# Two more pairs in the seven-product form in the down projection, and half of its loads on GpSimd's queue

## The chip, the cores and the metric

One core of a Trainium2 chip runs the whole kernel. The metric is the device time of one execution in microseconds (us), as a median of several runs. The engines are named as the profile names them: PE is TensorE's matmul, PEld its weight load, DVE is VectorE, ACT is ScalarE, POOL is GpSimd, SP is SyncE, which here only issues transfers. POOL issues transfers too.

## The reference, cut to what matters

One decoder layer over 256 tokens and 16 meta tokens with D_MODEL 2048: attention and retention heads from one input projection, an output projection, and a gated MLP with D_FF 5632. Only the MLP bears on this case. All of it is float32.

```
def conv_glu(u, w_gate, w_up, conv_w, w_down):
    g = u @ w_gate                      # then a causal depthwise conv of width 3
    ...
    return (jax.nn.silu(gc) * (u @ w_up)) @ w_down
```

`w_down` has 5632 rows and 2048 columns. Its product with the activations is the down projection, the last large product before the final norm.

## The kernel before, in words

Every large product runs on PE with each float32 operand split into a high and a low part of type fp32r: the high part is a cast (ACT, line 206, a copy into an fp32r tile), the low part is the difference (DVE, line 207, a subtraction). A product is then three matmuls, high by high, high by low and low by high (`triple`, lines 872 to 874). The 5632 rows of `w_down` are 44 blocks of 128, called k blocks.

**The gate and up stage** (loop over `f` in `range(NF)`, from line 794) makes the activations, one k block a step, and keeps their parts in `fhi` and `flo`. For the first `KP` = 2 x `NS` blocks the stage forms, after each odd `f`, four sums of the activations of two neighbouring blocks (lines 831 to 834), splits them, and stores three of them, high and low, to DRAM as `sd[p]` (384 KB, from POOL's queue, line 843). Between these steps it also prepares sums of the weights: `stage()` loads three blocks of a pair's weights (`ts`, 768 KB, POOL's queue, line 782), `sums()` makes two of the sums on DVE (lines 788 and 789) and stores both as `td[g, p]` (512 KB, POOL's queue, line 791), and stages the next. There are 2 x `NS` such steps. The staging tiles are the memory of `htok`, the residual, which is read back late in the stage, in halves.

**The down stage** (from line 927) works through two halves of the columns, `g` = 0 and 1, each of two blocks of 512 columns, for two halves of the tokens, 128 each. For two plain k blocks this takes 8 products of 128x128 by 128x512, that is 24 matmuls and two entries of prepared weights of 128x1024. For a pair of the first `KP` blocks, seven products do (a 2x2 by 2x2 scheme of Winograd's kind): 21 matmuls. A pair has four entries, called parts:

- `d`: two blocks of weights (128x1024), 2 products, one of which takes a stored sum of activations (`sf`)
- `u`: the two stored weight sums `td`, 2 products, both with `sf`
- `t`: a difference of what `d` and `td` loaded, made in place on DVE (line 218), 2 products
- `c`: one block of weights `sw` (128x512), 1 product

`down_order` mixes the parts with plain entries: a lead of plain entries (4 in the first half, 2 in the second), then the parts with the other plain entries spread between them, then a tail of plain entries (3, and 8 in the second half). With `NS` = 12 there are 12 pairs and 20 plain entries in each half. `NPL` is the number of plain pairs of blocks in one block of columns.

**Buffers and queues.** `ahead` loads up to 6 entries ahead and prepares (`prep`) up to 3 ahead in program order. Prepared weights lie in a ring of four: three buffers of `whi`/`wlo` and one of `wx`. Raw weights have five buffers. `sf` and `sw` have two each, for even and odd pairs. `load` issues four transfers for a pair, all from SP's queue: the two blocks of `d` (line 179), `sf` (line 180), `td` (line 181), `sw` (line 182). `keep` holds the marked instructions in program order; all others are placed by a scheduler that goes by its own timeline, so the order on each engine is fixed before the run but not by hand.

Small work for the residual is spread over the entries by `pump`: after the last part of a half, ten additions into `htok`; in the second half four products with the norm's weights (`weigh`, line 899) and one scaling of a norm tile (line 860), whose load `norm` is also from POOL's queue (line 855).

Of the kernel before, what the change touches and what calls it, by code (L numbers as in the profile page):

```python
# [10 lines left out]
F32 = mybir.dt.float32  # L11
# [29 lines left out]
NW = 512  # L41
# [3 lines left out]
LAM_INIT = 0.8 - 0.6 * math.exp(-0.3 * 0)  # L45
HK = KT // 2
HOLD = 6
NS = 12
KP = 2 * NS
NPL = (NF - KP) // 2  # L50
LEAD = [(4, 3), (2, HOLD + 2)]
# [44 lines left out]
def down_order():  # L96
# [3 lines left out]
    for g in range(2):  # L100
        plain = [("w", 2 * g + j, b) for j in range(2) for b in range(NPL)]
        parts = [("s", p, q) for p in range(NS) for q in PARTS]
        lead, tail = LEAD[g]
# [13 lines left out]
def trunk_kernel(ctx, tc, a, out):  # L117
    nc = tc.nc
# [23 lines left out]
    keep = tc.keep_in_program_order  # L142
# [18 lines left out]
    pools = {}  # L161
# [4 lines left out]
    def load(c):  # L166
        turn = (c - nw) % 5 if c >= nw else 0
        if turn == 3:
            t = pools["dn"].tile([P, D], F32, tag="sraw", name=f"raw{c}")
        elif turn == 4:  # L170
            t = big.tile([P, D], F32, tag="act1", name=f"raw{c}")
        else:
            t = wp.tile([P, D], F32, tag="raw", bufs=3, name=f"raw{c}")
        if c in mixed:
            g, p = divmod(mixed[c], NS)
            sf = big.tile([P, 6 * P], F32R, tag=f"act{2 + p % 2}a", name=f"sf{g}_{p}")
            sw = big.tile([P, NW], F32, tag=f"act{2 + p % 2}b", name=f"sw{g}_{p}")
            w = a["w_mix"][g, p]
            keep(nc.sync.dma_start(out=t[:, :2 * NW], in_=w[:, :2 * NW]))
            keep(nc.sync.dma_start(out=sf.bitcast(F32), in_=pools["sd"][p]))  # L180
            keep(nc.sync.dma_start(out=t[:, 2 * NW:], in_=pools["td"][g, p]))
            keep(nc.sync.dma_start(out=sw, in_=w[:, 2 * NW:3 * NW]))
            pools["sf"][g, p] = sf
            pools["sw"][g, p] = sw
        else:
            ins = nc.sync.dma_start(out=t, in_=chunks[c])
            if c >= nw:
                keep(ins)
        raw[c] = t

    def prep(hf):
# [18 lines left out]
        if c in mixed:  # L210
            g, p = divmod(mixed[c], NS)
            if s == "d":
# [75 lines left out]
    with tc.tile_pool(name="start", bufs=2) as st:  # L288
        acc = st.tile([P, 4, T], F32, name="acc", bufs=1)
        xrs, rws = [], []  # L290
        for c in range(4):
# [7 lines left out]
            for b, e in cuts:  # L299
                lead = c == 0 and b == 0  # L300
                (nc.scalar if lead else nc.sync).dma_start(
                    out=xr[:, b:e], in_=a["x"][:, 4 * c + b:4 * c + e])
# [140 lines left out]
    def gemm_q(idx, src, pumps):  # L443
        ps = unit(idx)
        for k, wh, wl in steps(idx, pumps):
            PE.matmul(ps[:, :NQ + 2], wh, src.cols(k, GO - 2, GL), start=(k == 0), stop=False)  # L446
            PE.matmul(ps[:, 4:NQ + 2], wh, src.cols(k, GL, GW), start=False, stop=False)  # L447
            PE.matmul(ps[:, 2:NQ + 2], wl, src.hi(k), start=False, stop=(k == KT - 1))  # L448
        edge = sp.tile([P, 2], F32, tag="edge", name=f"edge{idx}")
        S.copy(out=edge, in_=ps[:, 0:2])  # L450
        V.tensor_tensor(out=ps[:, 2:4], in0=ps[:, 2:4], in1=edge, op=ALU.add)
        return ps[:, 2:NQ + 2]

    def gemm_t(idx, src):
        ps = unit(idx)
        for k, wh, wl in steps(idx, 0):
            if k == KT - 1:
                PE.matmul(ps[:, :SEQ], wl, src.cols(k, GO + 2, GL), start=False, stop=False)
            PE.matmul(ps, wh, src.cols(k, GO + 2, GW), start=(k == 0), stop=(k == KT - 1))  # L459
            if k < KT - 1:  # L460
                PE.matmul(ps[:, :SEQ], wl, src.cols(k, GO + 2, GL), start=False, stop=False)  # L461
        return ps

    with ExitStack() as p1:
# [269 lines left out]
        for j in range(KT):  # L734
# [15 lines left out]
            for i in range(4):  # L750
                c = j * P + i * 32
                nc.sync.dma_start(
                    out=hd[:, c:c + 32].rearrange("(b t) f -> t b f", t=32),
                    in_=hb[i * 32:(i + 1) * 32].rearrange("t (b f) -> t b f", f=32))
# [9 lines left out]
    with ExitStack() as p2:  # L764
# [4 lines left out]
        fw = p3.enter_context(tc.tile_pool(name="fw", bufs=2))  # L769
        sd = [dp.tile([P, 6 * P], F32, name=f"sd{p}") for p in range(NS)]  # L770
        us = {}
        td = {}
        staged = []
        halfs = []
        order_g = [(g, p) for g in range(2) for p in range(NS)]

        def stage():
            n = len(td) + len(staged)
            if n < len(order_g):
                t = big.tile([P, 3, NW], F32, tag=f"htok{n % 2}", name=f"ts{n}")  # L780
                g, p = order_g[n]
                keep(nc.gpsimd.dma_start(out=t.rearrange("p a c -> p (a c)"),
                                         in_=a["w_mix"][g, p][:, NW:]))
                staged.append((g, p, t))

        def sums():
            g, p, t = staged.pop(0)
            keep(V.tensor_tensor(out=t[:, 2], in0=t[:, 0], in1=t[:, 2], op=ALU.subtract))
            keep(V.tensor_tensor(out=t[:, 1], in0=t[:, 2], in1=t[:, 1], op=ALU.add))
            o = td[g, p] = dp.tile([P, 2 * NW], F32, name=f"td{g}_{p}")  # L790
            keep(nc.gpsimd.dma_start(out=o, in_=t[:, 1:3].rearrange("p a c -> p (a c)")))
            stage()

        for f in range(NF):
            if f in (1, 2):
                stage()
            if staged and (f >= KP or f >= 4 and f % 2 == 0):
                sums()
            if f in (39, 41):
                m = (f - 39) // 2  # L800
                halfs.append(big.tile([P, D], F32, tag=f"htok{m}", name=f"htok{m}"))
                keep(nc.sync.dma_start(out=halfs[m], in_=hd[m * P:(m + 1) * P]))
            ps = gemm_q(idx, gs, 0)
            g = fw.tile([P, NQ], F32, tag="g", name=f"fg{f}")
            V.tensor_tensor(out=g, in0=ps[:, :NQ], in1=rstd2, op=ALU.mult)
            c = fw.tile([P, SEQ], F32, tag="c", name=f"fc{f}")
            V.tensor_scalar(out=c, in0=g[:, 0:SEQ], scalar1=cw[:, f, 0:1], scalar2=None,
                            op0=ALU.mult)
            for i in (1, 2):
                V.scalar_tensor_tensor(out=c, in0=g[:, i:i + SEQ], scalar=cw[:, f, i:i + 1],  # L810
                                       in1=c, op0=ALU.mult, op1=ALU.add)
            s = fw.tile([P, SEQ], F32, tag="s", name=f"fs{f}")
            S.activation(out=s, in_=c, func=AF.Silu)
            V.tensor_tensor(out=s, in0=s, in1=rstd2[:, 2:], op=ALU.mult)
            ps = gemm_t(idx + 1, gs)
            ul = fw.tile([P, SEQ], F32, tag="ul", name=f"ful{f}")
            S.copy(out=ul, in_=ps[:, SEQ:])
            u = ul
            V.tensor_tensor(out=u, in0=ps[:, :SEQ], in1=ul, op=ALU.add)
            V.tensor_tensor(out=u, in0=u, in1=s, op=ALU.mult)  # L820
            n = P if f < KP and f % 2 == 0 else SEQ
            S.copy(out=fhi[:, f, :n], in_=u[:, :n])
            V.tensor_tensor(out=flo[:, f, :n], in0=u[:, :n], in1=fhi[:, f, :n].bitcast(F32),
                            op=ALU.subtract)
            if f < KP and f % 2 == 0:
                us[f] = u
            elif f < KP:
                a1, a2 = us.pop(f - 1), u
                p = f // 2
                sm = fw.tile([P, 4, P], F32, tag="sm", bufs=1, name=f"sm{p}")  # L830
                V.tensor_tensor(out=sm[:, 0], in0=a1[:, P:], in1=a2[:, P:], op=ALU.add)
                V.tensor_tensor(out=sm[:, 1], in0=sm[:, 0], in1=a1[:, :P], op=ALU.subtract)
                V.tensor_tensor(out=sm[:, 2], in0=a1[:, :P], in1=a1[:, P:], op=ALU.subtract)
                V.tensor_tensor(out=sm[:, 3], in0=a2[:, :P], in1=sm[:, 1], op=ALU.subtract)
                s1 = fhi[:, f - 1, P:]
                S.copy(out=s1, in_=sm[:, 0])
                V.tensor_tensor(out=flo[:, f - 1, P:], in0=sm[:, 0], in1=s1.bitcast(F32),
                                op=ALU.subtract)
                sh = fw.tile([P, 2, 3, P], F32R, tag="sh", bufs=1, name=f"sh{p}")
                S.copy(out=sh[:, 0], in_=sm[:, 1:])  # L840
                V.tensor_tensor(out=sh[:, 1], in0=sm[:, 1:], in1=sh[:, 0].bitcast(F32),
                                op=ALU.subtract)
                keep(nc.gpsimd.dma_start(out=sd[p], in_=sh.rearrange("p a b c -> p (a b c)")
                                         .bitcast(F32)))
            idx += 2
# [309 lines left out]
```

## Time and profile before

| what | value |
|---|---|
| median of 3 runs | 1151.24 us (1151.17 to 1151.56) |
| profiled execution | 1151.3 us, its span 1149.5 us |
| granted TensorE clock | 0.998 |
| PE busy | 1138.5 us (99%) |
| DVE busy | 931.0 us (81%) |
| ACT busy | 605.6 us (53%) |
| gate and up stage | about 431 to 917 us of the span |
| down stage | from 916.66 us |

The span is from the first to the last instruction; the profiled execution took 1.8 us more than that. Busy shares are means over the whole span. A wait is put down to the engine that came last. The rows of windows give, for a stretch, the busy time of each engine with its number of instructions in brackets, the granted clock, the busy share of the DMA engines and the GB/s moved.

### The profile page before, as it was taken

How to read it: one execution, taken by the hardware profiler on the slowest of the kernel's cores; microseconds unless marked ns; L12 is line 12 of the kernel's file. 1: busy time of each engine (PE TensorE's matmuls, PEld its weight loads, DVE VectorE, ACT ScalarE, POOL GpSimd, SP SyncE). 2: the span in 40 equal slices, each digit the busy share in tenths (PEclk: the TensorE clock that was granted, in tenths of full speed). 3: DMA queues.
4: the chain of work that ended last, by engine and by line, in shares of the span. 5: the costliest groups of instructions: out<-in, count | busy, mean ns of one | idle time of the engine just before them, and what ended most of it. 6: DMA issues, size and time to landing. Idle time of an engine off the chain costs nothing.

```text
span 1149.5 us, 20662 instructions
## 1 busy us (share of the span) xinstructions
PE 1138.5 (99%) x7967; PEld 1065.6 (93%) x7967; DVE 931.0 (81%) x1738; ACT 605.6 (53%) x997; POOL 36.2 (3%) x84
## 2 busy tenths in 40 slices
PE   8999999999999999999999999999999999999997
PEld 7999999999999999999999999999999988888886
DVE  7898787667677769888888888888877778889996
ACT  7676665443345545444544444444444456656663
POOL 0000000000000000000000000100000000000000
PEclk9999999999999999999999999999999999999999
DMA  9644546565648875767867777888876588877981
GB/s 317 211 155 161 180 144 199 167 223 166 203 159 253 238 228 187 284 243 256 288 249 251 273 286 266 289 313 304 310 271 226 193 302 300 287 287 259 315 314 74
DMA packets 96018, 276.76 MB, mean 241 GB/s; under 512 B 43856, under 2 KB 52176, under 8 KB 74160
## 3 DMA queue, kind: packets, MB, share of 16 engines
q1 hardware_dynamic: 87616, 238.08, 59.9%
q0 software_dynamic: 8160, 37.23, 8.9%
q8 instruction: 62, 1.02, 0.3%
q14 instruction: 36, 0.29, 0.1%
q10 hardware_dynamic: 144, 0.14, 0.1%
HBM read 251.56 MB, written 23.86 MB: 240 GB/s over the span
## 4 chain that ended last, share of the span: by engine, by line
PE 98%; DMA 1%; ACT 0%; DVE 0%; issue 0%; SPq 0%; DVEq 0%; ACTq 0%
PE mm L459 14%; PE mm L448 10%; PE mm L446 10%; PE mm L447 10%; PE mm L438 7%; PE mm L439 7%; PE mm L440 7%; PE mm L461 7%; PE o L873 4%; PE o L874 4%; PE o L872 4%; PE x L872 2%; PE x L874 2%; PE x L873 2%; PE po L583 1%; DMA xr<-in_x_dram 1%
## 5 line engine op out<-in xcount | busy, mean ns | idle before, releaser
L206 ACT CAST whi<-raw 128x1024 fp32r<-128x1024 f32 x379 | 397.9, 1051 | 376.3 <-issue 90.7
L207 DVE TENSOR_TENSOR wlo<-raw,whi 128x1024 fp32r<-128x1024 f32 x379 | 462.0, 1222 | 131.6 <-ACT whi L206 124.7
L459 PE MATMUL mm<-g,whi 128*128 128x512 f32 x352 | 124.4, 392 | 0.0
L448 PE MATMUL mm<-g,wlo 128*128 128x258 f32 x352 | 99.4, 282 | 0.0
L438 PE MATMUL mm<-x,whi 128*128 128x272 f32 (+1 forms) x344 | 99.3, 289 | 0.0
L446 PE MATMUL mm<-g,whi 128*128 128x260 f32 x352 | 99.2, 282 | 0.0
L440 PE MATMUL mm<-x,wlo 128*128 128x272 f32 (+1 forms) x344 | 99.0, 288 | 0.0
L439 PE MATMUL mm<-x,whi 128*128 128x272 f32 (+1 forms) x344 | 98.9, 288 | 0.0
L461 PE MATMUL mm<-g,wlo 128*128 128x256 f32 x352 | 98.6, 280 | 0.0
L447 PE MATMUL mm<-g,whi 128*128 128x256 f32 x352 | 97.8, 278 | 0.0
L459 PEld LDWEIGHTS mm<-g,whi 128*128 128x128 f32 x352 | 66.1, 188 | 13.1
L446 PE MATMUL mm<-ys,whi 128*128 128x260 f32 x256 | 71.9, 282 | 0.0
L448 PE MATMUL mm<-ys,wlo 128*128 128x258 f32 x256 | 71.8, 281 | 0.0
L447 PE MATMUL mm<-ys,whi 128*128 128x256 f32 x256 | 70.7, 276 | 0.0
L447 PEld LDWEIGHTS mm<-g,whi 128*128 128x128 f32 x352 | 66.7, 189 | 1.9
L461 PEld LDWEIGHTS mm<-g,wlo 128*128 128x128 f32 x352 | 66.2, 188 | 0.0
L446 PEld LDWEIGHTS mm<-g,whi 128*128 128x128 f32 x352 | 66.1, 188 | 0.0
L448 PEld LDWEIGHTS mm<-g,wlo 128*128 128x128 f32 x352 | 66.0, 188 | 0.0
L439 PEld LDWEIGHTS mm<-x,whi 128*128 128x128 f32 x344 | 64.9, 189 | 0.0
L440 PEld LDWEIGHTS mm<-x,wlo 128*128 128x128 f32 x344 | 64.8, 189 | 0.0
L438 PEld LDWEIGHTS mm<-x,whi 128*128 128x128 f32 x344 | 64.8, 188 | 0.0
L873 PE MATMUL o<-wlo,fhi 128*128 128x512 f32 x149 | 58.0, 389 | 0.0
(404 smaller groups left out, 3060.6 us busy)
## 6 DMA issues: line engine op xcount, KB each, us to landing
raw<-in_w_in_dram SPq DMA_DIRECT2D x44, 1024.0 KB, 5.0
raw<-in_w_gate_dram SPq DMA_DIRECT2D x44, 1024.0 KB, 5.7
raw<-in_w_up_dram SPq DMA_DIRECT2D x44, 1024.0 KB, 5.4
raw<-in_w_down_dram SPq DMA_DIRECT2D x20, 1024.0 KB, 8.4
ts<-in_w_mix_dram POOLq DMA_DIRECT2D x24, 768.0 KB, 5.9
raw<-in_w_out_dram SPq DMA_DIRECT2D x16, 1024.0 KB, 5.3
td<-ts POOLq DMA_DIRECT2D x24, 512.0 KB, 6.6
raw<-in_w_mix_dram SPq DMA_DIRECT2D x24, 512.0 KB, 8.3
```

The source lines that it names most:

```text
L206: S.copy(out=hi[:, b:e], in_=src)
L207: V.tensor_tensor(out=lo[:, b:e], in0=src, in1=hi[:, b:e].bitcast(F32), op=ALU.subtract)
L438: PE.matmul(ps[:, :n], wh, xh, start=(k == 0), stop=False)
L439: PE.matmul(ps[:, :n], wh, xl, start=False, stop=False)
L440: PE.matmul(ps[:, :n], wl, xh, start=False, stop=(k == KT - 1))
L446: PE.matmul(ps[:, :NQ + 2], wh, src.cols(k, GO - 2, GL), start=(k == 0), stop=False)
L447: PE.matmul(ps[:, 4:NQ + 2], wh, src.cols(k, GL, GW), start=False, stop=False)
L448: PE.matmul(ps[:, 2:NQ + 2], wl, src.hi(k), start=False, stop=(k == KT - 1))
L459: PE.matmul(ps, wh, src.cols(k, GO + 2, GW), start=(k == 0), stop=(k == KT - 1))
L461: PE.matmul(ps[:, :SEQ], wl, src.cols(k, GO + 2, GL), start=False, stop=False)
L872: PE.matmul(o, ah, wh, start=start, stop=False)
L873: PE.matmul(o, ah, wl, start=False, stop=False)
```

## The change

`NS` goes from 12 to 14: two more pairs of k blocks use seven products, so each half of the columns has 14 pairs and 16 plain entries. `sf` and `sw` are loaded from POOL's queue; the weights of `d`, the sums `td` and the plain weights stay on SP's. In the gate and up stage the steps that sum weights are placed anew: two are staged at `f` = 0 and 1 (before: 1 and 2), and from `f` = 2 there is one in each step but every fourth, until all 28 are done (before: one in every second step from `f` = 4, and one in every step from `f` = 24, 24 in all). The two halves of the residual are read back at `f` = 41 and 42 (before: 39 and 41).

```
-NS = 12
+NS = 14
 KP = 2 * NS
 NPL = (NF - KP) // 2
...
             keep(nc.sync.dma_start(out=t[:, :2 * NW], in_=w[:, :2 * NW]))
-            keep(nc.sync.dma_start(out=sf.bitcast(F32), in_=pools["sd"][p]))
+            keep(nc.gpsimd.dma_start(out=sf.bitcast(F32), in_=pools["sd"][p]))
             keep(nc.sync.dma_start(out=t[:, 2 * NW:], in_=pools["td"][g, p]))
-            keep(nc.sync.dma_start(out=sw, in_=w[:, 2 * NW:3 * NW]))
+            keep(nc.gpsimd.dma_start(out=sw, in_=w[:, 2 * NW:3 * NW]))
...
         for f in range(NF):
-            if f in (1, 2):
+            if f < 2:
                 stage()
-            if staged and (f >= KP or f >= 4 and f % 2 == 0):
+            elif staged and (f % 4 != 3):
                 sums()
-            if f in (39, 41):
-                m = (f - 39) // 2
+            if f in (41, 42):
+                m = f - 41
                 halfs.append(big.tile([P, D], F32, tag=f"htok{m}", name=f"htok{m}"))
                 keep(nc.sync.dma_start(out=halfs[m], in_=hd[m * P:(m + 1) * P]))
```

## The prediction

> **What bounds the kernel now.** I read the page first: busy shares and the chain of waits.
>
> ```profile
> span 1149.5 us, 20662 instructions
> PE 1138.5 (99%) x7967; PEld 1065.6 (93%) x7967; DVE 931.0 (81%) x1738; ACT 605.6 (53%) x997; POOL 36.2 (3%) x84
> PE 98%; DMA 1%; ACT 0%; DVE 0%; issue 0%; SPq 0%; DVEq 0%; ACTq 0%
> ```
>
> PE is the chain. Fewer matmuls shorten the run as long as the others keep up; DVE's 81% is a mean, so I look at the stage that changes. The down stage starts here:
>
> ```profile
> 916.66 0.39 PE L872 MATMUL o<-whi,fhi 128*128 128x512 f32 x1
> 916.89 0.39 PE L873 MATMUL o<-wlo,fhi 128*128 128x512 f32 x1
> ```
>
> A lead of 4 plain entries is 48 matmuls, so the parts of the first half begin about 927.57 and end, 12 pairs and 12 plain entries later (one of the 13 comes after the last part), at 1017.33; those of the second half, with 9 plain entries between, run from 1033.65 to 1116.52. The two stretches, then the beginning of the second and 20 us of it, from the views of windows:
>
> ```profile
> 927.57:1017.33 89.76, 89.76 (x398) 74.32 (x396) 76.90 (x72) 56.49 (x62) 0.00 (x0) 1.00 0.88 317
> 1033.65:1116.52 82.87, 82.69 (x362) 67.26 (x361) 75.26 (x73) 53.34 (x60) 0.53 (x1) 1.00 0.83 295
> 1033.65:1056.65 23.00, 22.92 (x100) 18.43 (x99) 21.36 (x22) 15.84 (x19) 0.00 (x0) 1.00 0.70 250
> 1040.00:1050.00 10.00, 9.92 (x44) 7.93 (x43) 9.49 (x12) 6.83 (x8) 0.00 (x0) 1.00 0.69 224
> 1050.00:1060.00 10.00, 10.00 (x45) 8.03 (x44) 9.93 (x12) 5.25 (x7) 0.53 (x1) 1.00 0.96 373
> ```
>
> The third number after the length is DVE's share of the work. First stretch: 12 x 21 + 12 x 12 = 396 matmuls in 89.76 us, 0.2267 us each, with no hole (the 0.39 us of a row overlaps the next). Second: 252 + 108 = 360 matmuls are 81.60 us at that pace, the stretch took 82.87: PE lost 1.27 us. DVE is busy 91% there, 97% from 1040 to 1060, and there PE waits:
>
> ```profile
> 1049.06 0.39 PE L872 MATMUL x<-wx,fhi 128*128 128x512 f32 x1
> 1049.53 0.50 PE L872 MATMUL x<-whi,fhi 128*128 128x512 f32 x1
> ```
>
> 0.47 us from start to start instead of 0.23. So DVE is the engine next in line, in one stretch of the run.
>
> **The change part by part.**
>
> *Two more pairs.* In each half two pairs at 24 matmuls become two at 21: 12 matmuls fewer in all, 12 x 0.2267 = 2.72 us off PE. That is the whole gain; 0.2% of the run, about what a measurement can tell from no change, is 2.3 us.
>
> What a pair costs DVE is in these rows:
>
> ```profile
> L207 DVE TENSOR_TENSOR wlo<-raw,whi 128x1024 fp32r<-128x1024 f32 x33 | 39.8, 1221 | 6.2 <-ACT whi L206 5.7
> L218 DVE TENSOR_TENSOR raw<-raw 128x1024 f32<-128x1024 f32 x11 | 13.4, 1221 | 0.2
> L207 DVE TENSOR_TENSOR wlo<-sw,whi 128x512 fp32r<-128x512 f32 x10 | 6.8, 684 | 0.4 <-ACT whi L206 0.4
> 1097.64 1.22 DVE L207 TENSOR_TENSOR wlo<-raw,whi 128x1024 fp32r<-128x1024 f32 x1
> 1098.77 1.22 DVE L207 TENSOR_TENSOR wx<-raw,wx 128x1024 fp32r<-128x1024 f32 x1
> 1049.38 0.68 DVE L207 TENSOR_TENSOR wx<-sw,wx 128x512 fp32r<-128x512 f32 x1
> 1049.98 0.68 DVE L899 TENSOR_TENSOR htok<-htok,fn 128x512 f32<-128x512 f32 x1
> ```
>
> Back to back, a 1024-wide subtraction takes 1.14 us from start to start and a 512-wide one 0.60. A pair needs four of the first (`d`, `u`, `t` and the difference of line 218) and one of the second: 5.16 us, against 21 x 0.2267 = 4.76 on PE. A plain entry needs 1.14 against 2.72. So pairs run DVE into debt and plain entries pay it back, and the change adds two pairs and takes out four plain entries in each half, all from between the parts:
>
> - First half: PE 14 x 21 + 8 x 12 = 390 matmuls, 88.41 us (before 89.76, so -1.35). DVE 76.90 + 10.32 - 4.56 = 82.66, 93%.
> - Second half: 294 + 60 = 354 matmuls, 80.25 us. DVE 75.26 + 10.32 - 4.56 = 81.02, 101%.
>
> In the second half DVE becomes the bound, by 0.8 us even if it never idles. Its length lies between 81.0 (no idle time) and, at the idle share of its first 23 us (1.64 of 23.00), 81.0 / 0.929 = 87.2. Much of that idle time was waiting for a slot that PE still held, which goes when DVE is late; so I take the share of 1040 to 1060, where DVE was already behind: 0.58 of 20 us, 81.0 / 0.971 = 83.4, against 82.87 before: +0.55, ends -1.9 and +4.3. In the first half I add half of the 1.27 us that the old second half lost at 91% (four of its operations, `weigh`, aren't in this one): +0.6, ends 0 and +1.27.
>
> ACT gets 1.5 more casts a pair than two plain entries; at 53.34 of 82.87 us it covers them. If ACT were full, a pair would cost up to 3 x 1.05 + 0.62 us against 4.76, still less.
>
> *The steps that sum weights.* Four more `ts`, `td` and sums, two more pair sums, all in the gate and up stage, whose steps of 11.24 us look so:
>
> ```profile
> 439.50:450.70 11.20, 11.20 (x82) 10.52 (x81) 10.38 (x21) 5.08 (x9) 0.00 (x0) 1.00 0.53 188
> 450.70:462.00 11.30, 11.30 (x82) 10.62 (x81) 10.35 (x24) 6.33 (x13) 1.07 (x2) 1.00 0.63 222
> 462.00:473.20 11.20, 11.20 (x81) 10.52 (x81) 8.96 (x17) 5.32 (x10) 0.00 (x0) 1.00 0.71 259
> 473.20:484.50 11.30, 11.30 (x82) 10.62 (x81) 9.61 (x18) 5.62 (x10) 1.62 (x3) 1.00 0.88 318
> 743.00:754.20 11.20, 11.20 (x81) 10.52 (x81) 9.34 (x16) 5.11 (x9) 1.06 (x2) 1.00 0.81 303
> 889.10:900.40 11.30, 11.30 (x82) 10.61 (x81) 8.16 (x13) 5.22 (x9) 0.00 (x0) 1.00 0.54 187
> ```
>
> A step of sums costs DVE 9.34 - 8.16 = 1.2 us. The fullest late step gets 9.61 + 1.2 = 10.8 of 11.3: PE's 11.2 hides it. The sum now at `f` = 2 falls into the second window, 10.35 + 1.2 = 11.55, a quarter of a microsecond too much, which the third with its 8.96 takes up; uncovered it costs up to that 0.25 once. DMA is at 0.88 with sums already. Cost 0, ends 0 and 0.3. The later read of `htok` is wanted only after the last part of the first half, a hundred us on: 0.
>
> *Queues.* SP's queue stands at the head of `sf`, whose tile PE still reads, and all behind it waits:
>
> ```profile
> SPq L180 <- PE x L874: 112.5, 21, 14.0
> raw<-td SPq DMA_DIRECT2D x24, 512.0 KB, 5.8
> sf<-sd SPq DMA_DIRECT2D x24, 384.0 KB, 4.8
> sw<-in_w_mix_dram SPq DMA_DIRECT2D x24, 256.0 KB, 6.5
> ts<-in_w_mix_dram POOLq DMA_DIRECT2D x24, 768.0 KB, 5.9
> fn<-in_final_norm_dram POOLq DMA_DIRECT2D x2, 512.0 KB, 8.4
> ACT whi L206 <- DVE raw L218: 6.6, 4, 2.5
> ```
>
> After the change that wait stands on POOL's queue, and behind it there are `sw`, the norm tile `fn` and the next `sf`; SP runs ahead with `td` and the weights until its five buffers are full. What is worth having is an earlier `td`: where `u` and so line 218 are late, ACT waits for them (last row, 4 times in the second stretch). It is worth nothing to at most the 1.27 us that PE lost; I take 0, since DVE, not `td`, is full after the change.
>
> The price is `sf` from POOL. It can start when PE leaves `u` of the pair two back and is first read after 9 + 21 + 3 matmuls, 33 x 0.2267 = 7.5 us later where no plain entry lies between. POOL's nearest load in size took 5.9 us for twice the bytes: hidden. At the pace of `fn`, 8.4 us, it would be late by 0.9 us a pair.
>
> The Trainium skill speaks against the move twice. "SBUF — State Buffer" (section "SBUF: two separate sides") warns that descriptors of transfers from GpSimd's queue can't be written while VectorE holds the shared ports in its two-port modes; its section "Who interferes with whom" takes `tensor_tensor` out of that, as inferred. The next row shows that subtractions were not stretched by POOL's transfers:
>
> ```profile
> L207 DVE TENSOR_TENSOR wlo<-raw,whi x379: 1161/1225/1228, 28.4 to 1127.8; 128x1024 fp32r<-128x1024 f32 x190
> ```
>
> Minimum, median and maximum are within 6%, though POOL issued its 26 loads above in the same time. By the first warning `sf` would come late (a rival below), by the second not. "DMA: Bandwidth & Descriptors" (section "Issuing engines are not separate DMA queues") says that a second issuing engine saves issue time only; by it the move is worth about nothing, which is the value I took.
>
> *Sum:* -1.35 + 0.6 + 0.55 = -0.2 us on 1151.3, that of the profiled execution; the median of the runs, 1151.24, is the same to 0.1. Forecast 1151.0. Best end -1.35 - 1.9 = -3.2, worst end -1.35 + 1.27 + 4.3 + 0.3 = +4.5.
>
> **The rivals.**
>
> *DVE never idles* (faster). With `td` early, line 218 never holds ACT up, and the second stretch takes 81.0 to 81.8: -3.2 to -2.4, so 1148.0 to 1148.8. For it: the 6.6 us of waits for line 218 could go. Against: DVE idled 7.6 of 82.87 us before, and the `weigh` operations come in a clump of four within the first five pairs, where the change leaves one plain entry instead of two.
>
> *DVE idles as before* (slower). With a ring of four, a cast waits for PE's slot, and the subtraction for the cast; if this stays 7%, the second half takes 87.2 and the sum is -1.35 + 0.6 + 4.3 = +3.6, 1154.8. It decides from 4.9 us of idle time in that stretch (82.87 + 2.3 + 0.75 - 81.0). For it: both rows above with DVE over 90% show PE waits. Against: at 97% it lost only half a microsecond.
>
> *`sf` is late* (slower), at the start or in every pair.
>
> ```profile
> 914.76 0.33 SPq L180 DMA_DIRECT2D sf<-sd  x1
> 921.43 0.53 POOL L855 DMA_DIRECT2D fn<-in_final_norm_dram  x1 [75.67 <-DVE flo L823]
> L872 PEld LDWEIGHTS o<-whi,sf x3: 187/187/188, 927.6 to 940.0; 128*128 128x128 f32 x3
> ```
>
> The first `sf` was issued at 914.76 and read from 927.6; the first `fn` waits until 921.43 and takes 8.4 us. If it now stands ahead of `sf` in POOL's queue, `sf` lands not before 929.8, near 930.5 with its own bytes, and PE stops for some 2.5 us: about 1153.5. Against: the tile of `sf` is free 6 us before `fn` may start, so the scheduler likely puts `sf` first. If POOL's loads all need 8.4 us, 0.9 us in some 13 pairs is 12 us, near 1163.
>
> *No effect of the queues, pairs alone:* the forecast itself.
>
> **How the numbers follow.** Forecast, within 0.2% (1148.9 to 1153.5): 0.52. DVE never idles: 0.25. DVE idles as before: 0.15. `sf` late: 0.08. So faster 0.25, same 0.52, slower 0.23. The range reaches from inside the first rival to the second: 1148.3 to 1154.8; the forecast's own is 1149.5 to 1152.5.
>
> **What would show it.** Right: the stretch of the second half holds 354 matmuls in 82 to 84.5 us with DVE at 96% or more, that of the first half 390 in 88.4 to 89.7; every step of the gate and up stage still 11.24 us; SP's wait at line 180 gone and as long a one on POOL. Wrong: holes in PE ended by a landing of `sf` (POOL's queue); steps over 11.3 us; a second stretch at 80.3 us, which would mean that DVE's work moved out of it; or a scheduler that, with its new order, changes stages that I left at zero.

## The result, and the profile after

The changed kernel takes 1171.49 us (median of 4 runs, 1169.67 to 1172.21) against 1151.4 (1151.17 to 1151.65) for the kernel before on the same chip: a ratio of 1.0173, 95% interval 1.016 to 1.0187. The forecast was 1151.0 with a range to 1154.8. The profiled execution took 1169.67 us, 18.4 more than the one before, and all of the following is told of that one.

The page of the changed kernel, busy times and the chain's shares by engine:

```profile
span 1167.9 us, 20745 instructions
PE 1144.5 (98%) x7955; PEld 1063.8 (91%) x7955; DVE 947.9 (81%) x1770; ACT 611.8 (52%) x1009; POOL 72.0 (6%) x150
PE 91%; DVE 3%; DMA 2%; issue 2%; ACT 2%; POOL 0%; SPq 0%; DVEq 0%; ACTq 0%; POOLq 0%
```

The view of windows of the changed kernel: a part of the gate and up stage, the two stretches, the beginning of the first (length, busy us of PE, PEld, DVE, ACT, POOL, granted clock, DMA share, GB/s):

```profile
450.00:900.00 450.00, 450.00 (x3204) 422.85 (x3204) 376.67 (x666) 215.22 (x351) 36.36 (x68) 1.00 0.79 283
927.50:1025.44 97.94, 92.53 (x391) 73.37 (x390) 81.18 (x77) 58.29 (x65) 15.45 (x28) 0.98 0.85 313
1041.76:1134.71 92.95, 85.92 (x355) 66.06 (x354) 79.99 (x79) 55.49 (x63) 13.36 (x25) 0.98 0.69 251
927.50:943.45 15.95, 11.53 (x41) 8.02 (x40) 7.33 (x7) 5.37 (x7) 1.07 (x2) 0.89 1.02 414
```

PE has 12 matmuls fewer but is busy 6 us longer, and the chain is 91% PE instead of 98%. The gate and up stage is full as before, and the down stage begins at the same place (first parts at 927.50, before 927.57). The stretches, at PE's pace of 0.2267 us a matmul, from the first part to the end of the last:

| stretch | before | after | floor after | lost after |
|---|---|---|---|---|
| first half | 89.76 | 97.94 | 88.40 | 9.54 |
| second half | 82.87 | 92.95 | 80.24 | 12.71 |

The two floors together are 2.72 us lower; the losses rise from 1.27 to 22.25. Together that is 18.3, the whole of the 18.4.

**The start of the first half.** The timeline of POOL in the changed kernel (start, us, what, idle time before it and what ended it):

```profile
921.36 0.53 POOL L855 DMA_DIRECT2D fn<-in_final_norm_dram  x1 [64.43 <-DVE flo L823]
921.88 0.55 POOL L180 DMA_DIRECT2D sf<-sd  x1
922.42 0.54 POOL L182 DMA_DIRECT2D sw<-in_w_mix_dram  x1
```

The timeline of its PE at the same place:

```profile
928.64 0.39 PE L874 MATMUL o<-whi,flo 128*128 128x512 f32 x1
930.54 0.47 PE L872 MATMUL o<-whi,sf 128*128 128x512 f32 x1 [1.51 <-DMA sf<-sd]
934.51 0.50 PE L872 MATMUL x<-wx,fhi 128*128 128x512 f32 x1
936.99 0.50 PE L873 MATMUL x<-wx,fhi 128*128 128x512 f32 x1 [1.98 <-DVE wx L207]
```

Its waits on POOL's queue, and transfers with the median us to landing:

```profile
POOL sf L180 <- PE x L874: 147.8, 26, 19.8
...
raw<-td SPq DMA_DIRECT2D x28, 512.0 KB, 8.7
sf<-sd POOLq DMA_DIRECT2D x28, 384.0 KB, 6.0
```

The norm's load stands ahead of the first `sf`, which before was issued at 914.76 and now at 921.88. This `sf` lands at 930.4, PE stands still for it, and twice more behind it (starts 1.90, 2.48 and 1.25 us apart). The second and third hole are not waits for a transfer: DVE ends them, after it waited 5.3 us for a cast of ACT, which had waited 5.5 us for a slot of prepared weights that PE held while it stood. SP, no longer held by `sf`, issues its loads beside POOL's: the DMA engines are full (share 1.02), and `td`, which the move was to bring earlier, takes 8.7 us (the median of the run) in place of 5.8. The wait for the tile of `sf` stands on POOL now, 147.8 us. The first seven parts, 39 matmuls, take 15.94 us; 8.84 is their floor.

**The second half.** The changed kernel's waits from 1041.76 to 1134.71, ACT's and then DVE's (us, times, longest):

```profile
ACT whi L206 <- DVE raw L218: 12.4, 7, 2.9
ACT wx L206 <- DMA sw<-in_w_mix_dram: 6.2, 3, 4.5
...
DVE wx L207 <- ACT wx L206: 6.5, 4, 3.9
DVE wlo L207 <- ACT whi L206: 6.3, 7, 1.3
```

Waits for line 218 went from 6.6 us in 4 times to 12.4 in 7. The longest hole is that of a late `sw`, here in the timelines of ACT and PE:

```profile
1081.51 0.62 ACT L206 CAST wx<-sw 128x512 fp32r<-128x512 f32 x1 [4.53 <-DMA sw<-in_w_mix_dram]
...
1079.08 0.39 PE L874 MATMUL x<-whi,flo 128*128 128x512 f32 x1
1082.17 0.79 PE L872 MATMUL x<-wx,fhi 128*128 128x512 f32 x1 [2.70 <-ACT wx L206]
1082.77 0.63 PE L873 MATMUL o<-wlo,fhi 128*128 128x512 f32 x1
1083.19 0.63 PE L874 MATMUL o<-whi,flo 128*128 128x512 f32 x1
1083.62 0.63 PE L873 MATMUL o<-wlo,sf 128*128 128x512 f32 x1
```

Two windows of the changed kernel behind that hole (the column before the DMA share is the granted clock):

```profile
1082.20:1085.20 3.00, 3.00 (x7) 2.38 (x8) 2.95 (x4) 1.98 (x3) 0.00 (x0) 0.53 0.86 350
1085.20:1087.90 2.70, 2.70 (x13) 2.25 (x12) 2.33 (x2) 1.78 (x2) 0.63 (x2) 1.00 0.18 62
```

This `sw` was issued at 1073.32 and landed at 1081.40, and ACT's later casts, in order behind it, waited too. PE stood still 3 us, and then the matmuls start 0.43 us apart instead of 0.23 for 3 us more, with the granted clock at 0.53.

### The profile page after: what moved, and what is told of

Same layout as the page of the kernel before. It is cut to its first block, busy times and chain, and to the rows that moved or that the text cites. A ratio compares the mean times of both kernels' runs of the same rounds, so it can differ in the third digit from the quotient of the medians.

```text
span 1167.9 us, 20745 instructions
## 1 busy us (share of the span) xinstructions
PE 1144.5 (98%) x7955; PEld 1063.8 (91%) x7955; DVE 947.9 (81%) x1770; ACT 611.8 (52%) x1009; POOL 72.0 (6%) x150
## 3 DMA queue, kind: packets, MB, share of 16 engines
q8 instruction: 62, 1.02, 0.3%
## 4 chain that ended last, share of the span: by engine, by line
PE 91%; DVE 3%; DMA 2%; issue 2%; ACT 2%; POOL 0%; SPq 0%; DVEq 0%; ACTq 0%; POOLq 0%
PE mm L459 14%; PE mm L448 10%; PE mm L446 10%; PE mm L447 9%; PE mm L438 7%; PE mm L439 7%; PE mm L440 7%; PE mm L461 7%; PE o L873 3%; PE o L874 3%; PE o L872 3%; PE x L872 2%; PE x L873 1%; PE x L874 1%; DVE wlo L207 1%
## 5 line engine op out<-in xcount | busy, mean ns | idle before, releaser
L207 DVE TENSOR_TENSOR wlo<-raw,whi 128x1024 fp32r<-128x1024 f32 x383 | 467.1, 1222 | 135.9 <-ACT whi L206 130.0
L817 ACT COPY ful<-mm 128x256 f32<-128x256 f32 x44 | 16.4, 373 | 78.2 <-PE mm L459 75.7
```

The source lines that it names most:

```text
L207: V.tensor_tensor(out=lo[:, b:e], in0=src, in1=hi[:, b:e].bitcast(F32), op=ALU.subtract)
```

## The experiments

Each is told by the loss of the two stretches against their floors, since that is where the whole difference lies. Ratios are to the kernel before.

**1. The two parts of the change apart.** `e1_pairs_alone` is the changed kernel with the four loads of a pair on SP's queue; `e2_queues_alone` is the kernel before with only the queues changed.

```
e1:  -keep(nc.gpsimd.dma_start(out=sf.bitcast(F32), ...   +keep(nc.sync.dma_start(out=sf.bitcast(F32), ...
     -keep(nc.gpsimd.dma_start(out=sw, ...                +keep(nc.sync.dma_start(out=sw, ...
e2:  the same two lines of the kernel before, the other way round
```

> 14 pairs with all four loads from SP's queue as before. Theory Q (the loss comes from the queue move: sf and sw land late from POOL, behind fn at the start and behind each other later, and ACT's cast of c and PE stop): 1150 to 1154 us, the first stretch within 1 us of its 88.4 us floor, the second 82 to 85. Theory D (the loss comes from DVE's load of 101% in the second half, whatever the queue): only the 7 us of the start come back, 1162 to 1166 us, the second stretch still 90 us or more.

> 12 pairs, sf and sw from POOL's queue. Theory Q: slower by 8 to 17 us, 1159 to 1168 us, holes of PE at the first pair (some 7 us with the slow pace after them) and where ACT waits for sw. Theory D: 1151 to 1153 us but for the start, at most 1158 us; the second stretch 82 to 84 us as before.

Measured: e1 1163.33 us, ratio 1.01 (1.0085 to 1.0115); e2 1154.53, ratio 1.0027 (1.0017 to 1.0037). e1 loses 2.29 us in the first stretch and 12.96 in the second, e2 2.52 and 1.96. So both parts cost, and the second half's loss is there without the move of the queues, as theory D said. Apart they cost 11.7 and 2.9 us, together 20.1: some 5 us come only with both. The window of e1's second stretch and ACT's waits in it:

```profile
1034.80:1128.01 93.21, 85.73 (x356) 66.46 (x354) 80.19 (x79) 55.57 (x63) 0.53 (x1) 0.98 0.80 277
...
ACT whi L206 <- DVE raw L218: 12.0, 6, 2.9
...
ACT whi L206 <- DMA raw<-in_w_down_dram: 2.8, 1, 2.8
```

The waits for line 218 are those of the changed kernel. The last row is a price of the old queue: plain weights issued late, since SP waited at `sf`. The timeline of e2's PE shows the same late first `sf` as the changed kernel's:

```profile
930.61 0.47 PE L872 MATMUL o<-whi,sf 128*128 128x512 f32 x1 [1.78 <-DMA sf<-sd]
```

**2. The norm's load out of POOL's queue.** `e3_fn_from_sp`, `e13_first_fn_sp` and `e14_second_fn_sp` are the changed kernel with both norm loads, the first half's or the second half's issued by SP.

```
-            nc.gpsimd.dma_start(out=t, in_=a["final_norm"]...
+            nc.sync.dma_start(...)                           # e3
+            (nc.gpsimd if g else nc.sync).dma_start(...)     # e13
+            (nc.sync if g else nc.gpsimd).dma_start(...)     # e14
```

> The changed kernel with the norm tile fn loaded from SP's queue instead of POOL's. If fn ahead of the first sf and sw in POOL's queue is what stops PE from 928 to 943 us, that stretch (15.95 us for 8.84 us of matmuls) shrinks to under 11 us and the run to 1164 to 1167 us, under either theory. If the crowd of transfers after 921 us (SP's as much as POOL's) is the cause, the start stays at 13 us or more and the run at 1169 or more.

> The changed kernel with only the first half's final-norm load on SP's queue; the second half's stays in GpSimd's. Moving both (e3_fn_from_sp) took 4.7 us off the start of the pairs (15.94 to 11.22), 5.0 off the first stretch in all (97.94 to 92.92) and 5.1 off the second (92.95 to 87.87). If each norm load delays the pairs behind it in GpSimd's queue in its own half, the first stretch is 92 to 93 us here and the second stays at 92 to 93.5: median 1165.5 to 1167. If the second half's loss comes from the state in which the first half leaves the loads, both stretches are as in e3: 92.9 and 88, median 1160 to 1161.

> The changed kernel with only the second half's final-norm load on SP's queue. If each norm load delays its own half, the first stretch stays at 97 to 98.5 us and the second is 87.5 to 89: median 1166 to 1167. If the second half's loss comes from the state in which the first half leaves the loads, both stretches are as in the changed kernel, 98 and 93, and the median is 1171 to 1172.

| | us | ratio, 95% | start | first stretch lost | second stretch lost |
|---|---|---|---|---|---|
| after | 1171.49 | 1.0173 (1.016, 1.0187) | 15.94 | 9.54 | 12.71 |
| both on SP (e3) | 1160.51 | 1.0076 (1.0061, 1.0091) | 11.22 | 4.52 | 7.63 |
| the first (e13) | 1160.77 | 1.0086 (1.0071, 1.0102) | 11.23 | 4.56 | 8.67 |
| the second (e14) | 1165.15 | 1.0123 (1.0109, 1.0137) | 16.18 | 9.80 | 7.61 |

The first norm load ahead of the first pair's loads costs 4.7 us at the start: shown. e3's start of 11.22 missed "under 11", and its run is faster than the 1164 to 1167 expected, since the second stretch gained too. The 2.4 us still lost at its start go with the norm's load too, by the trace: `sf` goes out early now, but the norm's load stands at the head of SP's queue, and the first pair's weights come late behind it. The timelines of e3's POOL and SP, and a wait of its ACT from 920 to 943:

```profile
915.41 0.55 POOL L180 DMA_DIRECT2D sf<-sd  x1 [58.03 <-PE mm L461]
...
921.66 0.33 SPq L855 DMA_DIRECT2D fn<-in_final_norm_dram  x1
922.04 0.42 SPq L179 DMA_DIRECT2D raw<-in_w_mix_dram  x1
...
ACT whi L206 <- DMA raw<-in_w_mix_dram: 6.2, 1, 6.2
```

In the second half neither account holds alone: e13 went as the account of the state said, e14's stretches as that of each half's own load, and either move takes 4 to 5 us away. With the changed kernel's order the hole at 1079 comes about, and moving either load is enough to avoid it; why both are needed for it is not settled.

**3. The difference of line 218.** `e4_no_diff` is the changed kernel without it; `e5_diff_elsewhere` is e3 with a difference of the same size that the third part doesn't wait for.

```
e4:  -                V.tensor_tensor(out=two, in0=two, in1=t2, op=ALU.subtract)
e5:  +                V.tensor_tensor(out=raw[c][:, 2 * NW:], in0=raw[c][:, :2 * NW],
     +                                in1=raw[c][:, 2 * NW:], op=ALU.subtract)
```

> The changed kernel without the difference of line 218 (t is then prepared from what d loaded; the output is not the reference's). DVE has 1.14 us less in each pair, 32 us in all, and ACT no wait for it. Theory D: all but the start comes back, 1153 to 1159 us. Theory Q: the holes that late sf and sw make stay, 1162 to 1170 us.

> 14 pairs, sf and sw from POOL, fn from SP (1160.5 us, second stretch 87.9 us, DVE busy 79.8 of it), but the difference of line 218 is written over the sums td after their split, so t is prepared without waiting for it; the output is not the reference's. DVE's work is the same to the instruction. Theory D1 (DVE's throughput: it has more work than the stretch has time): the second stretch stays at 86 us or more and the run at 1158.5 to 1161. Theory D2 (the chain: ACT's cast of t waits for the difference, and DVE then for the cast, with a ring of four to hide it): the second stretch falls to 80.3 to 82.5 us and the run to 1152 to 1156.

Measured: e4 1154.53 us, ratio 1.0025 (1.0015 to 1.0035); e5 1152.54, ratio 1.0009 (1.0 to 1.0018). The window of e4's second stretch, and a wait of ACT in it:

```profile
1039.29:1119.53 80.24, 80.24 (x356) 66.44 (x354) 66.96 (x66) 56.75 (x62) 13.33 (x25) 1.00 0.79 288
...
ACT wx L206 <- DMA sw<-in_w_mix_dram: 0.3, 1, 0.3
```

The same stretch of e5, and ACT's largest wait in it:

```profile
1033.99:1117.63 83.64, 81.89 (x356) 65.98 (x354) 79.54 (x79) 57.11 (x64) 12.87 (x24) 1.00 0.75 277
...
ACT whi L206 <- PE o L873: 9.9, 10, 1.7
```

And of e3:

```profile
1037.58:1125.45 87.87, 84.36 (x356) 65.06 (x355) 79.81 (x79) 55.69 (x63) 12.83 (x24) 1.00 0.71 265
...
ACT whi L206 <- DVE raw L218: 11.8, 6, 2.9
```

Without the difference the stretch stands on its floor to a hundredth, and that with `sf`, `sw` and the norm on POOL as in the changed kernel: while DVE has room (67 of 80 us), ACT waits 0.3 us for `sw` and not 6.2, and PE not at all. The first stretch of e4 loses 6.92 us, all of it at the start (15.75 for 8.84). With the same work on DVE but nobody waiting for it (e5) the loss is 3.40; with the wait (e3) 7.63. So the stretch with the work alone loses 3.4 us, and the wait brings another 4.2. That is between the two theories (83.64 us; D2 said at most 82.5, D1 at least 86). The 4.2 are not the wait alone: without it the scheduler also placed the operations anew, and 23 of the 28 differences have another place in DVE's order than in e3.

**4. The difference earlier.** If the wait costs 4.2 us, line 218 sooner should give some of it back. `e6_diff_first` is e3 with the difference ahead of the second part's split in the program; `e9_diff_early` puts it with the first part's split; `e8_before_diff_first` is the kernel before with e6's edit; `e7_sf_last` is e1 with `sf` issued last of the four, and `e10_early_sp` is e7 with e9's edit.

```
e6, e8:  the subtraction of line 218 moved ahead of  halves(raw[c][:, 2 * NW:], 0, 2 * NW)
e9, e10: moved from  elif s == "u":  into  if s == "d":  behind its  halves(...)
e7:      keep(nc.sync.dma_start(out=sf...))  behind that of  sw
```

> The same base (14 pairs, sf and sw from POOL, fn from SP), with the difference of line 218 placed in program order ahead of the split of u instead of behind it; nothing is left out. D2: the cast of t then runs beside DVE's subtraction for u, the second stretch falls to 81 to 84 us, the run to 1152.5 to 1157. D1: no change, 1159 to 1162.

> 14 pairs, all four loads from SP's queue (1163.3 us), but sf is issued last of a pair's four, so its wait for PE holds up no td and no sw of its own pair. If the wait at the head of SP's queue is part of the loss with 14 pairs, 1157 to 1161 us, with no wait of ACT for weights or td in the second stretch. If the loss is DVE's and ACT's alone, 1162 to 1164.

> The kernel before with the difference of line 218 ahead of the split of u. D2: the second stretch loses less than its 1.26 us, 1150.0 to 1151.2 us. D1: no change, within 0.3 us of before.

> Fourteen pairs, B11 and activation sums on GpSimd's queue, final norm on SP's (as e3_fn_from_sp), and the difference of line 218 put into the program with a pair's first split instead of its second, so that in VectorE's order of instructions it stands in most pairs right behind the first split's subtraction. The same work on every engine. e3 ran 1160.51 us, with 7.63 us lost in the second half's stretch (87.87 us over a floor of 80.24). Chain theory (ScalarE's cast of the third part waits for the difference, then VectorE waits for that cast): ScalarE's waits for line 218 fall from 11.8 us to under 5, and the second stretch falls to 83 to 85 us; median 1156 to 1158. Throughput theory (VectorE's summed work of 80 us): nothing changes, since the work is the same: 87 to 88 us and 1160 to 1161. Queue theory (the late loads from GpSimd's queue): nothing changes either.

> Fourteen pairs with all four loads of a pair on SP's queue, B11 last of the four (as e7_sf_last, 1159.66 us, second stretch 90.17 us), and the difference of line 218 put into the program with the first split. Chain theory: ScalarE's waits for line 218 (11.2 us in e7) fall below 5 us and the stretch to 84 to 87 us; median 1154 to 1157. Throughput theory: 90 us and 1159 to 1160. Queue theory (what is late comes from the order of loads): 90 us too, the holes at the pair's loads unchanged.

| | us | ratio, 95% | first stretch lost | second stretch lost |
|---|---|---|---|---|
| e6 | 1160.76 | 1.008 (1.0066, 1.0094) | 4.50 | 8.40 |
| e7 | 1159.66 | 1.0069 (1.0054, 1.0085) | 2.37 | 9.93 |
| e8 | 1151.16 | 0.9999 (0.999, 1.0007) | 0.00 | 1.88 |
| e9 | 1160.29 | 1.0077 (1.0064, 1.009) | 4.46 | 7.76 |
| e10 | 1159.22 | 1.0073 (1.006, 1.0086) | 2.30 | 9.68 |

In the last two expectations, B11 is the block of `sw`; in e10, as in e7, the last of the four loads is `sf`, not B11. e7 bears on the queue and came out as expected: `sf` last on SP took the second stretch's loss from 12.96 to 9.93, with ACT's waits for `td` gone and those for plain weights at 0.7 us. The four others changed little, and tested almost nothing: the scheduler left the order on DVE nearly as it was. In e6 and e8 all differences have the place in DVE's order that they have in e3 and in the kernel before. In e9, against e3, and in e10, against e7, one of 28 has moved, ahead of one `weigh`; against the splits none has. So the forecasts of an earlier difference failed, but none of them was put to the test. One difference of e9 in the timelines of DVE and ACT, with ACT's largest wait in the second stretch:

```profile
1076.40 3.50 DVE L207 TENSOR_TENSOR wlo<-raw,whi 128x1024 fp32r<-128x1024 f32 x3
1079.93 1.23 DVE L216 TENSOR_TENSOR raw<-raw 128x1024 f32<-128x1024 f32 x1
1081.07 1.22 DVE L207 TENSOR_TENSOR wlo<-raw,whi 128x1024 fp32r<-128x1024 f32 x1
...
1081.19 1.05 ACT L206 CAST wx<-raw 128x1024 fp32r<-128x1024 f32 x1 [0.82 <-DVE raw L216]
...
ACT whi L206 <- DVE raw L216: 11.9, 6, 2.9
```

The same difference in e3, on DVE:

```profile
1076.95 3.49 DVE L207 TENSOR_TENSOR wlo<-raw,whi 128x1024 fp32r<-128x1024 f32 x3
1080.48 1.23 DVE L218 TENSOR_TENSOR raw<-raw 128x1024 f32<-128x1024 f32 x1
```

In both DVE works off a backlog: three splits without a break, then the difference (line 216 in e9). ACT waits 11.9 us in all in e9, 11.8 in e3. Whether the differences would do better at an earlier place in DVE's order stays open; these edits did not get them there, since these instructions are not among those that `keep` holds in program order.

**5. The difference on another engine.** `e11_diff_pool` is e10 with the difference on GpSimd.

```
-                V.tensor_tensor(out=two, in0=two, in1=t2, op=ALU.subtract)
+                nc.gpsimd.tensor_tensor(out=two, in0=two, in1=t2, op=ALU.subtract)
```

> As e10_early_sp, but the difference of line 218 is computed on GpSimd, whose queue has no pair's loads in this version. VectorE's work in the second stretch falls from about 80 us to 67 (as in e4_no_diff, 66.96), and the dependence of the third part on the difference stays. Throughput theory: the stretch falls near its floor as in e4, 80.2 to 82 us, median 1149.5 to 1152. Chain theory: it depends on how long one difference takes on GpSimd, which no run shows yet: up to about 4 us it is done before the cast of the third part wants it and the stretch is 80.2 to 83; at over 6 us the chain is longer than before and the stretch above 90 us, median above 1159. If the two engines disturb each other, VectorE's 1024-wide subtraction takes longer than its 1.16 us beside such an instruction.

Measured: 1180.35 us, ratio 1.0254 (1.024 to 1.0269). A group of DVE and one of POOL in its second stretch, and the window (groups: count, busy us, mean ns, idle time before them):

```profile
L207 DVE TENSOR_TENSOR wlo<-raw,whi 128x1024 fp32r<-128x1024 f32 x35 | 52.9, 1525 | 15.7 <-ACT whi L206 15.5
...
L216 POOL TENSOR_TENSOR raw<-raw 128x1024 f32<-128x1024 f32 x13 | 40.1, 3081 | 56.9 <-DVE wlo L207 40.3 <-DVE wx L207 16.5
...
1045.60:1145.42 99.82, 87.19 (x356) 66.17 (x354) 81.25 (x66) 55.55 (x63) 40.64 (x14) 0.98 0.71 255
```

The same group of DVE in e3:

```profile
L207 DVE TENSOR_TENSOR wlo<-raw,whi 128x1024 fp32r<-128x1024 f32 x35 | 42.3, 1220 | 6.5 <-ACT whi L206 6.1
```

One difference takes 3.08 us there, and DVE's splits of this group grow from 1.22 to 1.53 us as a mean, so 66 operations keep DVE as busy (81.25 us) as 79 did: the work was not taken off DVE, and the chain got 2 us longer. The expectation of a stretch near 80 us failed by the first of these; the second alone, 3.08 us, was inside its bound.

**6. More plain entries between the parts.** `e12_more_plain` is e3, `e15_before_more_plain` the kernel before, each with the second half's lead of two plain entries spread between the parts instead.

```
-LEAD = [(4, 3), (2, HOLD + 2)]
+LEAD = [(4, 3), (0, HOLD + 2)]     # e12 has 8 in place of HOLD + 2, the same number
```

> Fourteen pairs, queues as in e3_fn_from_sp, and the second half begins with its pairs at once instead of two plain entries, so that eight plain entries instead of six lie between the parts of pairs. The stretch from the first part to the end of the last then holds 378 matmuls (floor 85.68 us) instead of 354 (80.24). Each plain entry brings 12 matmuls (2.72 us of TensorE) for one subtraction of VectorE (1.16 us), so VectorE's surplus over TensorE falls by 3.1 us. If the loss is VectorE's work with the wait for the difference on top (7.63 us lost in e3), the stretch loses 4 to 5 us, and the loop's whole loss falls from 12.56 to 9 or 10; median 1157 to 1158. If the loss comes from each pair's own wait, whatever stands between the pairs, it stays at 7 to 8 us and the median at 1160 to 1161. If the second half's first loads come too late without the two plain entries ahead of them, a hole of 2 us or more appears at its first pair and the median is 1161 or more.

> The kernel before, with twelve pairs and its own queues, and the second half begins with its pairs at once, so that two more plain entries lie between the parts of pairs, as in e12_more_plain. Before loses 1.26 us in the second half's stretch (82.87 over a floor of 81.60), and the two plain entries take 3.1 us of VectorE's surplus over TensorE away (e12: the loss fell by 3.1). If this surplus is the cause there too, the stretch is on its floor, now 87.04, and the loop loses 0.0 to 0.3 us in place of 1.29: median 1149.9 to 1150.6. If the second half's first loads are late without the plain entries ahead, or the loss moves to the end as part of it did in e12, the median is 1151 to 1152.5.

Measured: e12 1158.74 us, ratio 1.0065 (1.0053 to 1.0078); e15 1153.19, ratio 1.0018 (1.0009 to 1.0027). The second stretch of e12:

```profile
1031.86:1122.09 90.23, 88.17 (x380) 70.38 (x379) 85.26 (x86) 59.57 (x71) 12.84 (x24) 1.00 0.79 282
```

And of e15:

```profile
1028.77:1118.99 90.22, 89.10 (x386) 71.62 (x384) 79.69 (x80) 56.45 (x68) 0.53 (x1) 1.00 0.80 283
```

e12: 378 matmuls, floor 85.68, lost 4.54 in place of 7.63, the 3.1 us of the expectation, but not for its reason. DVE's work against PE's floor did not fall: 85.26 us of 85.68 here, 79.81 of 80.24 in e3, because five of the additions into `htok`, which had run beside the lead, now lie in the stretch. What fell is DVE's idle time, 4.97 us against 8.06. So the same work costs less when plain entries stand between the parts instead of ahead of them, and the loss is not simply DVE's surplus over PE. The run gained only 1.8 us: behind the last part it is 1.5 us longer than e3, with a hole of 1.9 us at 1130.25 that DVE ends.

e15 missed: 3.18 us lost where before lost 1.27, 2.81 of them by 1061.5, in the first third (the first eight parts take 12.32 us for 11.56). That third, in the view of windows:

```profile
1028.77:1061.50 32.73, 31.69 (x133) 24.39 (x132) 29.22 (x32) 20.25 (x28) 0.53 (x1) 1.00 0.74 256
```

Its 132 matmuls need 29.92 us, and DVE is busy for 29.22: here too the additions came in. So with twelve pairs as well, PE loses time where DVE is nearly full for some 30 us, though the mean of the whole stretch is lower (79.69 of a floor of 87.04). None of the versions beats the kernel before.

## Why the prediction was wrong, point by point

- **PE, 2.72 us less: right.** e4's second stretch is exactly 354 matmuls long, and e4's first without its start too.
- **Gate and up stage, 0: right.** 450.00 us of PE in 450.00, and the down stage starts 0.07 us earlier than before.
- **DVE's work, 76.90 + 10.32 - 4.56 and 75.26 + 10.32 - 4.56: right to 1.5 us.** 81.18 us in the first stretch against 82.66 forecast, 79.99 in the second against 81.0. So in sum DVE's work stayed just under PE's floor of 80.24, where I had 101%.
- **The idle share of the second stretch, taken as 2.9%: the step that failed.** I chose it between "no idle time" and 7% because DVE was already behind in the rows I took it from, and argued that the waits would go when DVE is late. They went only in part: ACT's waits for a slot fell from 23.4 us to 18.8, while DVE's idle time rose from 7.6 to 13.0. The third part's cast waits for a DVE result, ACT's other casts stand in order behind it, and DVE then waits for ACT. These waits for line 218 went from 6.6 us in 4 times to 12.4 in 7: more of them, not longer ones. The stretch without disturbance from the norm's load (e3) took 87.87 us, with DVE idle for 8.06 of them, 9.2%. That is 0.7 us beyond the end 87.2 of my own bounds, near the rival "DVE idles as before", to which I gave 0.15. Even without the wait (e5) DVE idled 4.10 of 83.64 us, 4.9%; that 83.64 lies near my 83.4 is luck, since the work was 79.54 us and not 81.0. The waits of ACT do not give PE's loss by themselves: e15 has 16.9 us of them for line 218 and loses 3.18.
- **The first stretch, taken as 0.6 us lost: too small.** With the queues as before (e1) it is 2.29, outside my ends of 0 and 1.27; in e4, without the difference, it is 0 apart from the start. The mean of 93% for DVE hid fuller places: from 980 to 1000 us of the changed kernel DVE is busy for 19.12 of 20.00 us.
- **`sf` from POOL, taken as hidden: the other step that failed, at the start.** I argued that the scheduler likely puts `sf` ahead of `fn`, since its tile is free earlier. The row at 921.36 shows the opposite. The rival's mechanism was right and so was its landing (930.4 against "near 930.5", though `fn` took 7.0 us and not 8.4). Its price of 2.5 us was right with twelve pairs, where e2 loses 2.28 us at the start, but 7.1 were lost with fourteen: two more holes followed, as ACT and DVE had stood behind the slot that PE held. With twelve pairs a plain entry comes after four parts, with fourteen after seven; that this makes the difference is likely, but no run shows it. "Every pair late" did not come: of the 28 `sf` only that first one has PE waiting for it by the profile.
- **An earlier `td`, taken as 0: not refuted.** SP did run ahead, but `td` took 8.7 us instead of 5.8. ACT waits for no `td` in the second stretch, before or after; with fourteen pairs and the old queues (e1) it waits 1.8 us for `td` and 2.8 for plain weights, and the move took these waits away.
- **The warning of the Trainium skill that GpSimd's descriptors wait for VectorE in its two-port modes** ("SBUF — State Buffer", section "SBUF: two separate sides"), which I set aside, does not show here. In the changed kernel the four issues behind the norm's load followed each other at 0.53 to 0.54 us; what took 8 to 11 us was from issue to landing, with the DMA share at 1.02. The Trainium skill's rule that a second issuing engine saves issue time only ("DMA: Bandwidth & Descriptors", section "Issuing engines are not separate DMA queues") agrees in that `td` got slower, 8.7 us for 5.8, when more loads ran at once.
- **The sum.** Forecast: -1.35 + 0.6 + 0.55. Measured: -1.36 + 9.54 in the first half, -1.36 + 11.44 in the second. Of the 9.54, 7.1 are the start and 2.4 DVE. Of the 12.71 lost in the second, 3.40 are DVE's work (e5), 4.23 the wait for line 218 with the order that comes with it (e3 less e5) and 5.08 the hole at 1079 and its neighbours, which go with the norm's load (after less e3). Before lost 1.27 there. The last 5.08 need DVE's load too: e4, with the norm on POOL as in the changed kernel, loses 0.00. I had priced the slower rivals one at a time; here two of them came together, and the norm's load in the second half was a third that I had not named.

## What to carry to other kernels

When a change brings an engine near 100% in a stage, ask whether any engine waits for a result of that engine and feeds it again; if so, take the idle share from the worst place and not from the best; here even the worst (7.1%) was below what came (9.2% in e3). A load that is moved to another queue is placed behind whatever that queue issues at the same moment, so write out that queue's order at the start of the stage, and count the loads that the old queue will now issue at once. Moving the load that has to wait to another queue can shift the wait to that queue's loads, as in e3. Taking a little work off PE by giving more to the engine next in line needs plain work between the pieces: two plain entries put there gave 1.8 us of the run back with fourteen pairs (e12), and with twelve the same edit cost 1.9 (e15). And before a version is read as a test of an order, compare the order of the engine in the two traces: in e9 one of 28 differences had moved, and none against the splits.

## What the runs showed of the hardware

After a hole of about 3 us PE runs at half its pace for a while. In the changed kernel the matmuls after 1082.17 start 0.43 us apart for some 3 us, granted clock 0.53, then 0.23 again; the same follows the holes at 934.51 and 937.55, and in e1, five matmuls later, a hole of 2.83 us. Two smaller holes close together did it too: 1.45 and 1.53 us, 1.04 apart, in e4. After single holes the pace stays at 0.23, up to 2.16 us in e2. The hole of 3 us cost some 4 in all (2.9, and at least 5 matmuls at 0.20 more). The Trainium skill ("TensorE: Matmul & The Clock Gate", section "Wait — 56ns, not 53.3ns?") has 426.7 ns for a cold matmul of this width, which agrees; its section "What's actually happening" wants an idle window of about 3.4 us for that, and here 3.09 and 2.83 us of idle time between starts sufficed.

GpSimd arithmetic beside two-input subtractions on VectorE slowed the latter by a quarter as a mean (1.22 to 1.53 us in e11), while transfers issued by GpSimd did not (1.22 us in e3 too). "SBUF — State Buffer" of the Trainium skill (section "Who interferes with whom") says that a VectorE instruction with two SBUF inputs contends with GpSimd's reads; e11 agrees. The mean hides two kinds, here in e11's timelines of DVE and POOL:

```profile
1088.51 3.41 DVE L207 TENSOR_TENSOR wlo<-raw,whi 128x1024 fp32r<-128x1024 f32 x1
...
1088.13 2.71 POOL L216 TENSOR_TENSOR raw<-raw 128x1024 f32<-128x1024 f32 x1 [3.61 <-DVE wlo L207]
```

This split began 0.38 us behind the start of a difference and ended 1.08 us behind its end. Of the 61 splits in that stretch, 8 went so, all begun while a difference ran: 2.3 to 3.4 us long, and ended 1.08 us behind it, or 0.55 where they were 512 wide. The other 53 took 1.21 to 1.27 us, or 0.68 to 0.69, as without GpSimd. These stood still until the difference was done. Not each one that begins so does: at 1081.05 one took 1.21 us, and the difference beside it 3.85.
